# A third gate group by seven products, stick-breaking weights as products of sigmoids, and projections ahead of merges in one two-layer decoder kernel

## The chip, the cores and the metric

The kernel runs on one core of one Trainium2 chip. Such a core has a matrix engine (TensorE, PE in the profile; PEld are its weight loads), a vector engine (VectorE, DVE), a scalar engine with function tables (ScalarE, ACT), GpSimd (POOL), and SyncE (SP), which issues most DMAs. The metric is the device time of one execution in microseconds, and a lower one is better. The time before is the median of three runs.

## The reference

Two layers, each of a half-step feed-forward, a mixing of three branches, and a second half-step feed-forward, on 512 positions of width 1024. The mixing, cut to what matters here:

```python
def _stick_breaking_attention(q, k, v):            # 8 heads of 64
    z = einsum('bhqd,bhkd->bhqk', qb, k) * scale
    mask = key_pos[None, :] < q_pos[:, None]
    log_beta = log_sigmoid(z)
    log_not = where(mask, log_beta - z, 0.0)
    log_between = cumsum(log_not, axis=3, reverse=True) - log_not
    w = where(mask, exp(log_beta + log_between), 0.0)
    return w @ v

u = rmsnorm(h, mix_pre_g[l])
q_sb, k_sb, v_sb, q_fx, k_fx, v_fx, f_logit, q_mem = split(u @ w_in[l], ...)
o_sb = stick_breaking(q_sb, k_sb, v_sb)
log_f = log_sigmoid(f_logit + b_forget[l])
o_fx = forgetting(q_fx, k_fx, v_fx, log_f)         # softmax(z + c_q - c_k), c = cumsum(log_f)
o_mem = memory(q_mem, k_mem, v_mem)                # 4 heads of 128 over 256 memory rows
g_sb, g_fx, g_mem = split(sigmoid(u @ w_gate[l] + b_gate[l]), 3)
merged = g_sb * (o_sb @ w_br_sb[l]) + g_fx * (o_fx @ w_br_fox[l]) + g_mem * (o_mem @ w_br_mem[l])
h = h + rmsnorm(merged @ w_out[l], mix_post_g[l])
```

In words: the weight of a key in the stick-breaking branch is sigmoid(z) at that key times the product of 1 - sigmoid(z) = sigmoid(-z) over the keys between it and the query. `log_between` is the logarithm of that product.

## The kernel before

All large products are made from two parts: an operand is split into a high and a low part in a reduced format (`split`, and the weight units with tiles `wh_` and `wl_`), and `mm3` (L216 to L218) issues high by high, high by low and low by high. A split costs a cast on ACT (L190, or L193 with a scale) and a subtraction on DVE (L191, L194). A weight unit is 128 x 1024 elements.

Some products are made by blocks instead, with seven block products in place of eight: two rows of blocks by two columns, each a round of its own (`block_units`, `ORDER`, `FIRST`), on 256 columns at a time. The feed-forwards do so, and so do the gates of the first two branches (`SETS = (0, 1)`): `block_gates` forms the sums of the rounds, `settle` adds the bias and takes a tanh (sigmoid(x) is 0.5 + 0.5 tanh(x/2)), and the result is parked in DRAM in `gsave`. `merge` later reloads a 128 x 512 piece to a tile `ga` by a DMA of POOL (L1674), multiplies it into the branch's output projection `pb` (L1681) and adds it to `merged` (L1682). The gate of the memory branch (2) is made otherwise: `mem_gate` runs plain products of 512 columns (`pg`), then a sigmoid by Exp, a minimum, Ln, a max-add and Exp (L204 to L212), and multiplies it into `merged` (L1651), to which `mem_branch` copied the projection (L1637).

What runs when in the mixing is set by a queue of jobs `Q` in the order of `Q.add`. Heads are chains of steps woven into that queue: after each step a chain says how much PE work of the queue is to go by, `("wait", us)`, before it goes on. The order: gate rounds; four memory heads (pvm, ptm) woven with the last rounds; the projections `project` (pq, pk) and `project_v` (pv), with `mem_branch`, `mem_gate` and the merges, woven with eight stick heads and then eight forgetting heads, each started W_NEXT after the one before it; the merges of branch 1; then the output projection.

A stick head has three steps: the scores into three PSUM banks `zs` (L1305) and on them the chain of ACT and DVE passes to the weights `ts` (L1310 to L1322); after W_SB0 = 12.0 us of queue the ten transposes `pts` (L1291) into banks of the same pool ("z", four banks), split to a tile; after W_SB1 = 4.7 us eight products with v, `pvs` (L1278). A forgetting head is alike: `zf` (L1349 to L1357), row maximum, Exp with sum, reciprocal and scaling (`pf`, L1359 to L1363), `ptf`, `pvf`. It needs the cumulative sums of the forget gates, `forget_cumsum` (transposes `pfl` L1438, ACT passes, a scan, copies to `cs`), which `fox_pre` scales to `qk` (L1340). The pass tiles all come from one pool of five 128 x 512 tiles (`tmp`).

The ACT passes need function tables: Tanh stands in one, Exp and Ln in another; `tables` loads one ahead of its use.

Of the kernel before, what the change touches and what calls it, by code (L numbers as in the profile page):

```python
# [17 lines left out]
P = 128  # L18
# [4 lines left out]
def kernel(  # L23
# [73 lines left out]
    begins16 = cst.tile([P, S], BF16, name="begins16")  # L97
# [19 lines left out]
    nbgate = cst.tile([P, L, 3 * ND], F32, name="nbgate")  # L117
# [3 lines left out]
    def vectors():  # L121
# [9 lines left out]
        nc.scalar.mul(nbgate[:, :, :2 * ND], bias[:, :, :2 * ND], 0.5)  # L131
        nc.scalar.mul(nbgate[:, :, 2 * ND:], bias[:, :, 2 * ND:], -1.0)
# [8 lines left out]
    def more_constants():  # L141
# [9 lines left out]
        later(nc.vector.memset(t2[:], 1.0))  # L151
        nc.gpsimd.affine_select(out=t3[:], in_=t2[:], pattern=[[-1, S]], compare_op=ALU.not_equal,
                                fill=0.0, base=S - P - 1, channel_multiplier=1)
        later(nc.vector.tensor_copy(begins16[:], t3[:]))
# [46 lines left out]

    def log1p_exp(t, z, bias=0.0):

        nc.scalar.activation(t, z, AF.Exp, bias=bias)  # L204
        nc.vector.tensor_scalar(t, t, 2.0 ** 62, None, ALU.min)
        nc.scalar.activation(t, t, AF.Ln, bias=one_t[:t.shape[0]])

    def sigmoid_neg(t, z, bias):

        log1p_exp(t, z, bias=bias)  # L210
        nc.vector.scalar_tensor_tensor(t, z, bias, t, ALU.add, ALU.max)
        nc.scalar.activation(t, t, AF.Exp, scale=-1.0)  # L212
# [325 lines left out]
    gsave = nc.dram_tensor("gsave", (2, 2, 2, P, D), F32, kind="Internal").ap()  # L538
# [756 lines left out]
    def stick_head(q, k, value, j, ot, name, ahead):  # L1295
# [5 lines left out]
        for rows, pz in zip(banks, pzs):  # L1301
# [6 lines left out]
            zr, t = pz[:, :w], tmp(f"t{name}_{rows[0][0]}")  # L1308

            nc.scalar.activation(t[:, :w], zr, AF.Abs)  # L1310
            nc.scalar.activation(t[:, :w], t[:, :w], AF.Exp, scale=-1.0)
            nc.scalar.activation(t[:, :w], t[:, :w], AF.Ln, bias=one_t[:])
            nc.vector.scalar_tensor_tensor(t[:, :w], zr, 0.0, t[:, :w], ALU.max, ALU.add)
            for i, at in rows:
                n = (i + 1) * P
                back = t[:, at + n - 1:at - 1 if at else None:-1]

                nc.vector.tensor_tensor_scan(back, begins16[:, S - 1:S - 1 - n if n < S else None:-1], back, 1e30,
                                             ALU.mult, ALU.add)
                ptile[i] = t[:, at:at + n]  # L1320
            nc.vector.tensor_tensor(t[:, :w], zr, t[:, :w], ALU.subtract)
            nc.scalar.activation(t[:, :w], t[:, :w], AF.Exp)  # L1322
# [97 lines left out]
    W_SB0, W_SB1 = 12.0, 4.7  # L1420
# [6 lines left out]
    SETS = (0, 1)  # L1427
# [27 lines left out]
    def mixing(l, src, ks, vs, values, dst):  # L1455
# [96 lines left out]
        def project(br, p):  # L1552
            base = br * 1536
            marks["before", br, p] = len(Q.jobs)
            for x, off, scale in (("q", 0, 0.125), ("k", 512, None)):
                un1 = Unit(w_in[l], 0, ND, base + off + p * P, P, f"{x}{l}_{br}_{p}")
                marks[br, p] = Q.add([un1], lambda x=x, un1=un1, scale=scale: proj((x, br, p), un1, scale))
                if (br, p, x) == (1, FOX[0], "k"):
                    Q.add([], lambda: forget_cumsum(l, st["fl"], st))
# [13 lines left out]
        def settle(br, i, j, banks=None):  # L1573

            t = st.pop(("c", i, j))
            for m in range(4):
                c = HALVES[m % 2]
                d = br * ND + 4 * j + m
                nc.scalar.activation(t[:, m // 2, c], t[:, m // 2, c] if banks is None else banks[m // 2][:, c], AF.Tanh,
                                     bias=nbgate[:, l, d:d + 1], scale=-0.5 if j else 0.5)  # L1580
            nc.scalar.dma_start(gsave[br, i, j], t[:].rearrange("p e q -> p (e q)"))

        def block_gates(br, n, uns, top):

            nm = f"g{l}_{br}"
            if n == 2:
# [18 lines left out]
            if n == 0:  # L1605
                t = st["p0", br] = stile([P, 2, S], "rs", f"c{nm}_00", F32)
                for e in range(2):
                    nc.scalar.copy(t[:, e], pts[e][:])
                return
# [17 lines left out]
        def mem_branch(dp):  # L1627
            ub = wpair(w_br_mem[l], NP, dp * 256, f"wb{l}_2_{dp}")

            def run():  # L1630
                if dp == 0:
                    st["merged"] = [stile([P, 2, S], "f", f"mg{l}_{i}", F32) for i in range(ND // 2)]
                    st["ms"] = []
                for m in range(2):
                    pb = pbank("mm", f"pb{l}_2_{2 * dp + m}")
# [351 lines left out]
```

## Time and profile before

| | |
|---|---|
| median of 3 runs | 2362.73 us (2361.63 to 2364.0) |
| profiled execution | 2364.89 us |
| its span, first to last instruction | 2362.8 us |
| granted TensorE clock, mean | 0.998 |
| stick stage of the first layer | about 510 to 660 us of the span |
| forgetting stage of the first layer | about 660 to 790 us |
| ACT table loads in the program | 18 |

The profile gives the busy time of each engine and the share of the span, a chain of work followed back from the last instruction, and for each engine what it stood idle for. A row of the timeline is: start, duration, engine, line, operation, output from inputs, shape, and the idle time before it with what ended it. Neighbouring instructions of one kind are one row with their count. Durations of products on PE overlap, so their price is read from start to start. In a row of groups stand the total and the mean duration in nanoseconds, then the idle time before them.

### The profile page before, as it was taken

How to read it: one execution, taken by the hardware profiler on the slowest of the kernel's cores; microseconds unless marked ns; L12 is line 12 of the kernel's file. 1: busy time of each engine (PE TensorE's matmuls, PEld its weight loads, DVE VectorE, ACT ScalarE, POOL GpSimd, SP SyncE). 2: the span in 40 equal slices, each digit the busy share in tenths (PEclk: the TensorE clock that was granted, in tenths of full speed). 3: DMA queues.
4: the chain of work that ended last, by engine and by line, in shares of the span. 5: the costliest groups of instructions: out<-in, count | busy, mean ns of one | idle time of the engine just before them, and what ended most of it. 6: DMA issues, size and time to landing. Idle time of an engine off the chain costs nothing.

```text
span 2362.8 us, 32037 instructions
## 1 busy us (share of the span) xinstructions
PE 2339.0 (99%) x11944; PEld 1988.2 (84%) x11944; DVE 1827.1 (77%) x2443; ACT 1483.3 (63%) x2406; POOL 261.6 (11%) x290
## 2 busy tenths in 40 slices
PE   9999999999999999999999999999999999999998
PEld 8788889988878788888888888899888887888887
DVE  8766978767887887769787679777688887866696
ACT  6665766657765465566665566656677554656574
POOL 1101101001022111101011110010011120110110
PEclk9999999999999999999999999999999999999999
DMA  8866858632223576759586767585322236876682
GB/s 244 236 179 176 225 183 247 168 100 76 85 81 98 189 221 169 189 152 261 166 220 172 188 184 233 188 235 148 107 64 81 81 99 206 224 184 179 175 226 98
DMA packets 237407, 398.03 MB, mean 168 GB/s; under 512 B 12458, under 2 KB 86466, under 8 KB 236740
## 3 DMA queue, kind: packets, MB, share of 16 engines
q1 hardware_dynamic: 197472, 312.06, 40.5%
q0 software_dynamic: 37472, 75.54, 17.6%
q10 hardware_dynamic: 2308, 8.39, 0.9%
q8 instruction: 94, 1.54, 0.3%
q14 instruction: 61, 0.50, 0.1%
HBM read 372.87 MB, written 23.07 MB: 168 GB/s over the span
## 4 chain that ended last, share of the span: by engine, by line
PE 91%; DVE 4%; ACT 2%; DMA 1%; issue 1%; POOL 0%; DVEq 0%; SPq 0%; POOLq 0%; ACTq 0%
PE ptc L216 5%; PE ptc L218 5%; PE ptc L217 5%; PE pta L216 5%; PE pta L218 5%; PE pta L217 5%; PE pdc L218 3%; PE pdc L217 3%; PE pdc L216 3%; PE pda L218 3%; PE pda L217 3%; PE pda L216 3%; PE g L216 2%; PE g L218 2%; PE g L217 2%; PE pb L216 2%
## 5 line engine op out<-in xcount | busy, mean ns | idle before, releaser
L191 DVE TENSOR_TENSOR wl_tc<-ktc,wh_tc 128x1024 fp32r<-128x1024 f32 x80 | 97.7, 1223 | 63.3 <-ACT wh_tc L190 63.1
L191 DVE TENSOR_TENSOR wl_ta<-kta,wh_ta 128x1024 fp32r<-128x1024 f32 x80 | 97.6, 1223 | 57.6 <-ACT wh_ta L190 57.5
L190 ACT CAST wh_tc<-ktc 128x1024 fp32r<-128x1024 f32 x80 | 84.1, 1054 | 67.8 <-PE ptc L218 48.0
L218 PE MATMUL pta<-wh_ta,aga 128*128 128x512 f32 x320 | 124.7, 390 | 1.6 <-DVE aga L191 1.6
L216 PE MATMUL pta<-wh_ta,aga 128*128 128x512 f32 x320 | 125.2, 392 | 0.0
L216 PE MATMUL ptc<-wh_tc,agc 128*128 128x512 f32 x320 | 125.1, 393 | 0.0
L190 ACT CAST wh_ta<-kta 128x1024 fp32r<-128x1024 f32 x80 | 84.1, 1053 | 65.3 <-PE pta L218 41.7
L218 PE MATMUL ptc<-wh_tc,agc 128*128 128x512 f32 x320 | 124.7, 390 | 0.0
L217 PE MATMUL pta<-wl_ta,aga 128*128 128x512 f32 x320 | 124.6, 389 | 0.0
L217 PE MATMUL ptc<-wl_tc,agc 128*128 128x512 f32 x320 | 124.6, 389 | 0.0
L191 DVE TENSOR_TENSOR wl_ta<-raw_ta,wh_ta 128x1024 fp32r<-128x1024 f32 x58 | 70.9, 1224 | 43.2 <-ACT wh_ta L190 43.0
L191 DVE TENSOR_TENSOR wl_tc<-raw_tc,wh_tc 128x1024 fp32r<-128x1024 f32 x56 | 68.5, 1224 | 45.3 <-ACT wh_tc L190 45.3
L190 ACT CAST wh_ta<-raw_ta 128x1024 fp32r<-128x1024 f32 x58 | 60.9, 1052 | 46.9 <-PE pta L218 38.0
L190 ACT CAST wh_tc<-raw_tc 128x1024 fp32r<-128x1024 f32 x56 | 59.0, 1053 | 47.9 <-PE ptc L218 36.6
L216 PE MATMUL ptc<-wh_tc,us_b 128*128 128x512 f32 x224 | 87.7, 391 | 0.2
L216 PE MATMUL pda<-wh_da,aa 128*128 128x512 f32 x224 | 87.5, 391 | 0.0
L216 PE MATMUL pdc<-wh_dc,ac 128*128 128x512 f32 x224 | 87.5, 391 | 0.0
L218 PE MATMUL ptc<-wh_tc,us_b 128*128 128x512 f32 x224 | 87.2, 389 | 0.0
L217 PE MATMUL ptc<-wl_tc,us_b 128*128 128x512 f32 x224 | 87.2, 389 | 0.0
L218 PE MATMUL pda<-wh_da,aa 128*128 128x512 f32 x224 | 87.2, 389 | 0.0
L217 PE MATMUL pda<-wl_da,aa 128*128 128x512 f32 x224 | 87.2, 389 | 0.0
L217 PE MATMUL pdc<-wl_dc,ac 128*128 128x512 f32 x224 | 87.2, 389 | 0.0
(613 smaller groups left out, 7930.3 us busy)
## 6 DMA issues: line engine op xcount, KB each, us to landing
raw_ta<-in_ffn_w_gate_dram SPq DMA_DIRECT2D x44, 512.0 KB, 4.5
raw_wg<-in_w_gate_dram SPq DMA_DIRECT2D x44, 512.0 KB, 3.9
raw_tc<-in_ffn_w_gate_dram SPq DMA_DIRECT2D x44, 512.0 KB, 4.2
raw_da<-in_ffn_w_down_dram SPq DMA_DIRECT2D x42, 512.0 KB, 3.8
raw_dc<-in_ffn_w_down_dram SPq DMA_DIRECT2D x42, 512.0 KB, 3.4
kta<-in_ffn_w_up_dram SPq DMA_DIRECT2D x40, 512.0 KB, 5.9
ktc<-in_ffn_w_up_dram SPq DMA_DIRECT2D x40, 512.0 KB, 6.1
raw_wo<-in_w_out_dram SPq DMA_DIRECT2D x24, 512.0 KB, 4.1
```

The costliest lines, as they stand in the source:

```text
L190: both = [nc.scalar.copy(h_ap, src)]
L191: make = lambda: nc.vector.tensor_tensor(l_ap, src, h_ap.bitcast(F32), ALU.subtract)
L216: nc.tensor.matmul(pt, lh, rh, start=start, stop=False, skip_group_check=free)
L217: nc.tensor.matmul(pt, lh, rl, start=False, stop=False, skip_group_check=free)
L218: nc.tensor.matmul(pt, ll, rh, start=False, stop=stop, skip_group_check=free)
```

## The change

It has three parts. First, `SETS` becomes (0, 1, 2): the memory branch's gates are a third group by seven products, parked in `gsave` like the others; `mem_gate`, `mem_branch` and the two helpers of their sigmoid go, and `merge(2, ...)` starts `merged` by multiplying the reloaded gate with the bank. Second, a stick head takes two sigmoids of the scores on ACT, sigmoid(-z) to `as` and sigmoid(z) to `ts`, runs a multiplying scan backwards over `as` and multiplies `ts` with it, block by block; POOL clears one column of each block. Third, the order: W_SB0 is 7.0, `project_v` stands ahead of the merges, branch 0's merges are spread otherwise over the forgetting heads, and `forget_cumsum` is called from the last stick head's chain with a table load of its own.

```diff
@@ stick_head
+        rest = [stile([P, 2, S], "rs", f"a{name}_{x}", F32) for x in range(2)]
...
-            zr, t = pz[:, :w], tmp(f"t{name}_{rows[0][0]}")
+            zr, a, t = pz[:, :w], rest[x // 2][:, x % 2], tmp(f"t{name}_{rows[0][0]}")
-            nc.scalar.activation(t[:, :w], zr, AF.Abs)
-            nc.scalar.activation(t[:, :w], t[:, :w], AF.Exp, scale=-1.0)
-            nc.scalar.activation(t[:, :w], t[:, :w], AF.Ln, bias=one_t[:])
-            nc.vector.scalar_tensor_tensor(t[:, :w], zr, 0.0, t[:, :w], ALU.max, ALU.add)
+            nc.scalar.activation(a[:, :w], zr, AF.Sigmoid, scale=-1.0)
+            nc.scalar.activation(t[:, :w], zr, AF.Sigmoid)
             for i, at in rows:
                 n = (i + 1) * P
-                back = t[:, at + n - 1:at - 1 if at else None:-1]
-                nc.vector.tensor_tensor_scan(back, begins16[:, S - 1:S - 1 - n if n < S else None:-1], back, 1e30,
+                back = a[:, at + n - 1:at:-1]
+                nc.gpsimd.memset(t[:, at + n - 1:at + n], 0.0)
+                nc.vector.tensor_tensor_scan(back, back, ends16[:, S - 2:S - n - 1 if n < S else None:-1], 0.0,
                                              ALU.mult, ALU.add)
+                nc.vector.tensor_tensor(t[:, at:at + n - 1], t[:, at:at + n - 1], a[:, at + 1:at + n], ALU.mult)
                 ptile[i] = t[:, at:at + n]
-            nc.vector.tensor_tensor(t[:, :w], zr, t[:, :w], ALU.subtract)
-            nc.scalar.activation(t[:, :w], t[:, :w], AF.Exp)
...
-    W_SB0, W_SB1 = 12.0, 4.7
+    W_SB0, W_SB1 = 7.0, 4.7
-    SETS = (0, 1)
+    SETS = (0, 1, 2)
@@ merge
+                if br == 2 and dp == 0:
+                    st["merged"] = [stile([P, 2, S], "f", f"mg{l}_{i}", F32) for i in range(ND // 2)]
...
-                    nc.vector.scalar_tensor_tensor(a[:], a[:], 1.0, banks[m][:], ALU.add, ALU.mult)
-                    nc.vector.tensor_tensor(md, md, a[:], ALU.add)
+                    nc.vector.scalar_tensor_tensor(md if br == 2 else a[:], a[:], 1.0, banks[m][:], ALU.add, ALU.mult)
+                    if br != 2:
+                        nc.vector.tensor_tensor(md, md, a[:], ALU.add)
@@ mixing
-                if (br, p, x) == (1, FOX[0], "k"):
-                    Q.add([], lambda: forget_cumsum(l, st["fl"], st))
...
-        for one in todo[0] + todo[1][:2]:
+        for one in todo[0] + todo[1] + todo[2][:3]:
             marks["tri"] = Q.add(*one)
-        for one in todo[1][2:]:
-            marks["sets"] = Q.add(*one)
+        for one in todo[2][3:]:
+            Q.add(*one)
...
+            if i in (2, 5):
+                project_v(*heads[4 if i == 2 else 6])
+                marks.setdefault("forget", len(Q.jobs))
             if br == 0:
-                mem_branch(i)
-                for dp in ((0,), (1,), (), (2, 3))[i]:
-                    mem_gate(dp)
+                marks["mem"] = merge(2, w_br_mem, i)
             else:
-                if i == NP:
-                    marks["sb"] = len(Q.jobs)
-                merge(0, w_br_sb, i - NP)
-            if i in (2, 4):
-                project_v(*heads[i + 2])
+                for dp in ((0,), (1,), (), (2, 3))[i - NP]:
+                    marks.setdefault("sb", len(Q.jobs))
+                    merge(0, w_br_sb, dp)
...
-                            tables("natural_log_exp_and_others")
+                            tables("sigmoid_and_others")
...
+                    if kind == "pe" and n == NH - 1 and steps == 1:
+                        Q.until(marks["forget"])
+                        tables("natural_log_exp_and_others")
+                        yield from (("pe", x) for x in forget_cumsum(l, st["fl"], st))
+                    if kind == "pe" and steps == 2:
+                        pre(n + 1)
```

In the compiled program PE has 7944 products of 512 columns and 2980 of 256 afterwards, where it has 8328 and 2308 before; per layer that is 192 wide ones fewer and 336 narrow ones more. ACT has 20 table loads for 18. Outside the mixing the order of PE is the same in both.

The names in the excerpts below carry the layer, the branch's head pair, the head and the bank (`ts0_1_0_3` is layer 0, pair 1, head 0, row block 3) and at the end a running number. On DVE, between a stick head's scores and the splits of its transposes (`order` prints a scan as SCALAR_TENSOR_TENSOR with `begins16` or `ends16`), there stand before, from the second bank's subtraction on:

```order
L1321 TENSOR_TENSOR ts0_1_0_2_5165<-zs0_1_0_2_5151,ts0_1_0_2_5165 128x384
L191 TENSOR_TENSOR wl_wb0_2_1_0_5084<-raw_wb0_2_1_0_4736,wh_wb0_2_1_0_5083 128x1024
L1282 TENSOR_TENSOR ss0_0_1_5195<-pvs0_0_1_5186,ss0_0_1_5195 64x512
L1313 SCALAR_TENSOR_TENSOR ts0_1_0_1_5177<-zs0_1_0_1_5152,ts0_1_0_1_5177 128x384
L205 TENSOR_SCALAR ga0_2_0_5200<-ga0_2_0_5200 128x512
L194 SCALAR_TENSOR_TENSOR wl_wg0_2_1_0_5090<-raw_wg0_2_1_0_4742,wh_wg0_2_1_0_5089 128x1024
L1318 SCALAR_TENSOR_TENSOR ts0_1_0_1_5177<-begins16_75,ts0_1_0_1_5177 128x256
L1318 SCALAR_TENSOR_TENSOR ts0_1_0_1_5177<-begins16_75,ts0_1_0_1_5177 128x128
L191 TENSOR_TENSOR o0_0_0_4151<-ss0_0_1_5195,o0_0_0_4151 64x512
L1321 TENSOR_TENSOR ts0_1_0_1_5177<-zs0_1_0_1_5152,ts0_1_0_1_5177 128x384
```

In the changed kernel DVE has at that place, for the whole chain of the same head:

```order
L1305 SCALAR_TENSOR_TENSOR as0_1_0_0_5569<-as0_1_0_0_5569,ends16_75 128x511
L1307 TENSOR_TENSOR ts0_1_0_3_5573<-ts0_1_0_3_5573,as0_1_0_0_5569 128x511
L1305 SCALAR_TENSOR_TENSOR as0_1_0_0_5569<-as0_1_0_0_5569,ends16_75 128x383
L1305 SCALAR_TENSOR_TENSOR as0_1_0_1_5570<-as0_1_0_1_5570,ends16_75 128x255
L1307 TENSOR_TENSOR ts0_1_0_2_5581<-ts0_1_0_2_5581,as0_1_0_0_5569 128x383
L1307 TENSOR_TENSOR ts0_1_0_1_5591<-ts0_1_0_1_5591,as0_1_0_1_5570 128x255
L1305 SCALAR_TENSOR_TENSOR as0_1_0_1_5570<-as0_1_0_1_5570,ends16_75 128x127
L1269 TENSOR_TENSOR ss0_0_1_5609<-pvs0_0_1_5600,ss0_0_1_5609 64x512
L190 TENSOR_TENSOR wl_q0_0_3_5529<-raw_q0_0_3_5193,wh_q0_0_3_5528 128x1024
L1307 TENSOR_TENSOR ts0_1_0_1_5591<-ts0_1_0_1_5591,as0_1_0_1_5570 128x127
```

The gate passes `ga` and the gate's weight split `wl_wg` are gone from among the head's passes; a split of the next pair's query weights and the sum of the previous head's output stand there.

On ACT, at the forget gates, before (two of the last stick head's passes follow the chain's first three, `fa`):

```order
L190 CAST k_1_2_6051<-pk_1_2_6002 64x512
L1442 ACTIVATE fa_6063<-pfl_6058,bfor 8x512
L1443 ACTIVATE fa_6063<-fa_6063 8x512
L1444 ACTIVATE fa_6063<-fa_6063,one_t 8x512
L1637 COPY mg_3_5054<-pb_2_6_6076 128x512
L190 CAST k_1_2_6051<-pk_1_2_6002 64x512
L1310 ACTIVATE ts_3_1_3_6099<-zs_3_1_3_6094 128x512
L1310 ACTIVATE ts_3_1_2_6109<-zs_3_1_2_6095 128x384
L1449 CAST cs_6070<-fb_6064 8x512
```

And afterwards ACT has, behind the sigmoids of the last stick head:

```order
L1299 ACTIVATE as_3_1_1_6304<-zs_3_1_1_6302 128x384
L1300 ACTIVATE ts_3_1_1_6325<-zs_3_1_1_6302 128x384
L1685 ACT_TABLE_LOAD
L1428 ACTIVATE fa_6340<-pfl_6335,bfor 8x512
L1429 ACTIVATE fa_6340<-fa_6340 8x512
L1430 ACTIVATE fa_6340<-fa_6340,one_t 8x512
L189 CAST wh_k_1_3_6287<-raw_k_1_3_6024 128x1024
L1435 CAST cs_6347<-fb_6341 8x512
```

The forget gates moved from ahead of the last head's scores to behind them, with a table load in front.

On PE, at the last forgetting head (pair 1, head 1), before, from the larger banks' scores to the transposes:

```order
L1356 MATMUL zf0_1_1_3_7445<-k0_1_1_7201,q0_1_1_7114 128x512
L1357 MATMUL zf0_1_1_3_7445<-qk0_1_1_7328 128x512
L1356 MATMUL zf0_1_1_2_7444<-k0_1_1_7201,q0_1_1_7114 128x384
L1357 MATMUL zf0_1_1_2_7444<-qk0_1_1_7328 128x384
L1278 MATMUL pvf0_1_0_7478<-ptf0_1_0_7401,v0_1_0_0_6681 128x512
L1278 MATMUL pvf0_1_0_7478<-ptf0_1_0_7401,v0_1_0_0_6681 128x384 x2
L1278 MATMUL pvf0_1_0_7478<-ptf0_1_0_7401,v0_1_0_1_6757 128x256 x4
L1291 MATMUL ptf0_1_1_0_7494<-ident_65,pf0_1_1_0_7474 128x128
```

And afterwards, from the smallest bank's scores, which are now the last, to the transposes:

```order
L1342 MATMUL zf0_1_1_0_7596<-k0_1_1_7385,q0_1_1_7349 128x256
L1343 MATMUL zf0_1_1_0_7596<-qk0_1_1_7469 128x256
L1265 MATMUL pvf0_1_0_7632<-ptf0_1_0_7528,v0_1_0_0_6990 128x512 x2
L1265 MATMUL pvf0_1_0_7632<-ptf0_1_0_7528,v0_1_0_0_6990 128x384 x2
L1265 MATMUL pvf0_1_0_7632<-ptf0_1_0_7528,v0_1_0_1_7071 128x256 x4
L203 MATMUL pb0_1_1_7591<-o0_1_3_6493,wh_wb0_1_0_0_7294 128x512
L204 MATMUL pb0_1_1_7591<-o0_1_3_6493,wh_wb0_1_0_0_7294 128x512
L205 MATMUL pb0_1_1_7591<-o0_1_3_6493,wl_wb0_1_0_0_7295 128x512
L203 MATMUL pb0_1_1_7591<-o0_1_0_6490,wh_wb0_1_0_0_7294 128x512
L204 MATMUL pb0_1_1_7591<-o0_1_0_6490,wh_wb0_1_0_0_7294 128x512
L205 MATMUL pb0_1_1_7591<-o0_1_0_6490,wl_wb0_1_0_0_7295 128x512
L1278 MATMUL ptf0_1_1_0_7654<-ident_65,pf0_1_1_0_7628 128x128
```

The two smaller banks' scores stood further ahead before; now all four come together, and six products of the merge that stood ahead of them stand behind the eight pvf.

62 lines of the change are left out of this document (17 added, 45 removed).

## The prediction

> **What bounds the kernel now.** I read the shares of the engines first, then the chain that ended last, then TensorE's waits.
>
> ```profile
> span 2362.8 us, 32037 instructions
> PE 2339.0 (99%) x11944; PEld 1988.2 (84%) x11944; DVE 1827.1 (77%) x2443; ACT 1483.3 (63%) x2406; POOL 261.6 (11%) x290
> ...
> PE 91%; DVE 4%; ACT 2%; DMA 1%; issue 1%; POOL 0%; DVEq 0%; SPq 0%; POOLq 0%; ACTq 0%
> ```
>
> TensorE (PE) is busy nearly throughout and holds 91% of the chain. So two things count: how long its own instructions take, and the few microseconds in which it stands still. The waits of PE name the second part:
>
> ```profile
> PE ptf L1291 <- DVE pf L1363: 6.4, 4, 2.4
> PE zs L1305 <- DVE pts L191: 2.4, 4, 0.9
> PE pts L1291 <- ACT ts L1322: 2.1, 2, 1.0
> ...
> PE zf L1349 <- DVE ptf L191: 1.4, 2, 0.7
> ...
> PE pvs L1278 <- ACT mg L1637: 0.9, 2, 0.5
> PE zf L1349 <- DVE pts L191: 0.3, 2, 0.2
> ...
> PE pb L216 <- ACT o L190: 0.2, 1, 0.2
> ```
>
> (Totals over both layers, the number of times, the longest.) Three rows that lie outside the mixing are left out. What is shown is 13.7 us: 5.7 in the stick stage (zs 2.4, pts 2.1, pvs 0.9, and the 0.3 behind its last head), 7.8 in the forgetting stage (ptf 6.4, zf 1.4), and 0.2. No change to VectorE (DVE) or ScalarE (ACT) can bring more than this 13.7 while PE's own work stays.
>
> **The change part by part.**
>
> *The third gate group.* The compiled program has per layer 192 products of 512 columns fewer on PE, and 336 of 256 columns more (seven rounds of 48). Their prices stand in the timeline of before, from the start of the first to the start behind the last:
>
> ```profile
> 375.99 0.28 PE L216 MATMUL g<-us_a,wh_wg 128*128 128x256 f32 x1
> ...
> 393.26 0.40 PE L216 MATMUL pqm<-us_a,wh_qm 128*128 128x512 f32 x1
> ```
>
> ```profile
> 556.87 0.40 PE L216 MATMUL pg<-us_a,wh_wg 128*128 128x512 f32 x1
> ...
> 562.32 0.39 PE L216 MATMUL pq<-us_a,wh_q 128*128 128x512 f32 x1
> ```
>
> The first pair encloses 144 narrow products: 17.27 / 144 = 0.1199 us each. The second encloses 24 wide ones: 5.45 / 24 = 0.2271. The 0.28 and 0.39 in the rows are durations of overlapped instructions and no price. Over two layers: 384 x 0.2271 = 87.2 removed, 672 x 0.1199 = 80.6 added, so **-6.6 us**. An eighth of the columns goes, but half a wide product would be 0.1136 and a narrow one costs 0.1199, so only 7.6% of 87.2 is left.
>
> The Trainium skill ("TensorE: Matmul & The Clock Gate", section "Back-to-back issue gap") speaks against this part: it gives sustained spacings of some 81 ns at 128 columns and 131 ns at 512, and on a line between them 256 columns would cost 98 ns, three quarters of a wide product; by these figures (an estimate) the change would add 672 x 0.098 - 384 x 0.131 = 15.6 us. The trace has 0.1199 beside 0.2271, a ratio of 0.53, in the very loop that is to be repeated, and decides. The Trainium skill's other formula in that section, N/2.4 + 2.5 ns, gives 109 and 216 ns and with them -9.5.
>
> Three of the new rounds lengthen the straight piece ahead of the memory heads; the last four take the place among these heads that the second group's last four have now. What they need besides PE is seen where the first two groups run now:
>
> ```profile
> core 0: us, PE busy (x) PEld busy (x) DVE busy (x) ACT busy (x) POOL busy (x), PEclk, DMA share, GB/s
> 404.00:440.00 36.00, 36.00 (x256) 33.85 (x255) 25.87 (x26) 22.49 (x31) 5.68 (x6) 1.00 0.87 220
> 510.00:585.00 75.00, 73.81 (x355) 61.65 (x355) 56.27 (x85) 55.00 (x98) 3.23 (x6) 1.00 0.27 74
> 585.00:660.00 75.00, 74.53 (x414) 65.03 (x414) 60.68 (x98) 57.89 (x109) 13.69 (x17) 1.00 0.26 75
> ```
>
> In 404 to 440 PE is busy for all 36.00 us, with DVE at 0.72, ACT at 0.62 and the DMA engines at 0.87. So the group's combinations, parkings and fetches cost nothing there. If the DMA cover failed, its 0.13 of room says how thin it is; the fetches stand some 20 us ahead in the queue, so I price it at 0. Settling, reloading and the four `memset`s of a head are on engines with room (POOL 11%; its nearest row, a 128x128 memset, is not even on the chain). I take 0 for them.
>
> *The stick heads.* Next the cost of the chain between the score products (zs) and the transposes (pts), by lines and forms of DVE:
>
> ```profile
> L1681 DVE SCALAR_TENSOR_TENSOR ga<-ga,pb 128x512 f32<-128x512 f32 x32 | 21.2, 679 | 5.3 <-PE pb L218 2.9 <-DMA ga<-gsave 2.4
> L1318 DVE TENSOR_TENSOR_SCAN ts<-begins,ts 128x512 f32<-128x512 bf16 x16 | 19.5, 1217 | 0.1
> L1321 DVE TENSOR_TENSOR ts<-zs,ts 128x384 f32<-128x384 f32 x32 | 17.5, 548 | 0.3
> ...
> L1318 DVE TENSOR_TENSOR_SCAN ts<-begins,ts 128x384 f32<-128x384 bf16 x16 | 15.0, 935 | 0.0
> L211 DVE SCALAR_TENSOR_TENSOR ga<-pg,nbgate,ga 128x512 f32<-128x512 f32 x16 | 12.0, 749 | 3.7 <-ACT ga L206 3.6
> L1313 DVE SCALAR_TENSOR_TENSOR ts<-zs,ts 128x512 f32<-128x512 f32 x16 | 11.1, 692 | 28.2 <-ACT ts L1312 28.0
> ...
> L1651 DVE TENSOR_TENSOR mg<-mg,ga 128x512 f32<-128x512 f32 x16 | 11.0, 687 | 0.8 <-ACT ga L212 0.7
> L1318 DVE TENSOR_TENSOR_SCAN ts<-begins,ts 128x256 f32<-128x256 bf16 x16 | 10.9, 678 | 0.1
> L1321 DVE TENSOR_TENSOR ts<-zs,ts 128x512 f32<-128x512 f32 x16 | 10.8, 674 | 0.0
> ...
> L205 DVE TENSOR_SCALAR ga<-ga 128x512 f32<-128x512 f32 x16 | 6.7, 417 | 3.1 <-ACT ga L204 3.1
> L191 DVE TENSOR_TENSOR pts<-pts,pts 128x256 fp32r<-128x256 f32 x16 | 6.6, 415 | 0.1
> L1318 DVE TENSOR_TENSOR_SCAN ts<-begins,ts 128x128 f32<-128x128 bf16 x16 | 6.4, 400 | 0.0
> L191 DVE TENSOR_TENSOR pts<-pts,pts 128x128 fp32r<-128x128 f32 x16 | 4.5, 280 | 0.0
> ```
>
> Per head the max-add goes (0.692 + 2 x 0.546 = 1.78 us on DVE). The four scans stay (1.217 + 0.935 + 0.678 + 0.400 = 3.23; I take the multiplying scan at the price of the adding one). The three subtractions (1.77) become four multiplications by row block (0.67 + 0.55 + 0.42 + 0.28 = 1.92). On ACT four passes of each bank become two, and the one at the chain's end goes.
>
> In return PE leaves less room. Before, 14.1 us of PE work stand between zs and pts; now 8 zs, 8 pvs and 27 wide products. The first two are read from
>
> ```profile
> 535.60 1.45 PE L1305 MATMUL zs<-k,q 128*128 128x512 f32 x8
> ...
> 554.28 1.45 PE L1305 MATMUL zs<-k,q 128*128 128x512 f32 x8
> 555.57 1.46 PE L1278 MATMUL pvs<-pts,v 128*128 128x512 f32 x8
> 556.87 0.40 PE L216 MATMUL pg<-us_a,wh_wg 128*128 128x512 f32 x1
> ```
>
> as 1.29 + 1.30, so 2.59 + 27 x 0.2271 = 8.7 us. The chain needs 0.5 for the first bank, about 0.3 of latency, 0.49 for a sigmoid (I take the Abs pass's duration, its row is below), then 3.23 + 1.92 less seven overlaps of some 0.08: about 5.9 us, in all **6.0 to 6.5**. 2.2 to 2.7 us remain for what else stands in DVE's queue; the order puts two or three passes there, of which a weight split (1.22) is the largest. In most heads that just fits, in two or three of a layer's eight it does not.
>
> ```profile
> L1310 ACT ACTIVATE ts<-zs x48: 463/487/600, 511.4 to 1826.5; 128x384 f32<-128x384 f32 x32, 128x512 f32<-128x512 f32 x16
> ```
>
> So of the stick stage's 5.7: the wait for ACT's last pass (2.1) and that for the copy of the memory branch (0.9) go with their instructions. The waits for a free z bank (2.4 + 0.3) arose where the splits of pts stood behind the gates' passes on DVE, which are gone, while a reload-and-multiply and a weight split remain: I take half, 1.35. For new waits ahead of pts: nothing at the least; at the most, if every head misses by one weight split less the room, about 1.2 x 16 = 19. I take 0.3 us at three heads a layer, about 1.65 in all, since DVE's load hardly rises. Before, a head lasts 18.7 us (its zs start at 535.60 and 554.28) with DVE at 0.78, the mean of the two windows above: 14.6 us. Without the plain gates (8 a layer, so one a head, of 24 wide products) it lasts 18.7 - 5.45 = 13.2, and on DVE go 1.78 - 0.15 in the head itself, 0.42 + 0.75 + 0.69 of the gate and about 1.2 for its weight split, while 0.68 comes: 10.6, a load of 0.80. Sum 3.0, so **-2.7 us**.
>
> *The forget gates.* They run after the last stick head's sigmoids, with one table load of 1.28 us more a layer on ACT.
>
> ```profile
> 646.12 0.60 PE L1438 MATMUL pfl<-ident,fl 128*8 128x128 f32 x4
> ...
> 657.07 0.49 DVE L1340 TENSOR_SCALAR qk<-cs,sel 40x512 fp32r<-40x512 f32 x1 [1.44 <-POOL cs L1452]
> ```
>
> The chain from pfl to the scaled cumulative sums takes 11.4 us now; 12.7 with the table load, and the order leaves 17.8 us of PE work up to the first zf that needs it. Cost 0, with some 4 to 5 us of cover; without it every us counts.
>
> *The forgetting stage and its end.* Before, the last head's largest two banks are computed right ahead of only seven pvf, and then PE stands:
>
> ```profile
> 783.17 1.22 PE L1278 MATMUL pvf<-ptf,v 128*128 128x512 f32 x7
> 786.77 2.04 PE L1291 MATMUL ptf<-ident,pf 128*128 128x128 f32 x10 [2.39 <-DVE pf L1363]
> ```
>
> Now all four banks come in one piece, the largest first, and eight pvf (1.3) and six wide products (1.36) stand between the last zf and ptf, 2.66 us in place of some 1.1. So ptf's wait falls by about 1.6 to 1.7 a layer; I take 6.4 to 3.0 for both layers. The gap ahead of zf of one other head gets shorter (2.0 us for 3.4), so zf goes from 1.4 to 2.4. Together **-2.4 us**; bounds: nothing gained, and 7.8.
>
> *Sum.* -6.6 - 2.7 - 2.4 = -11.7. Against the profiled execution (2364.89, its span 2362.8) that gives 2353.2; this execution lies 2.2 above the median, so 2362.73 - 11.7 = **2351.0 us**.
>
> **The rivals.**
> R1: *the waits only move.* Denser stick heads wait as long as the old ones: 13.7 stays, only -6.6 counts: 2356.1. For it: PE's room per head falls from 14.1 to 8.7 us. Against it: two of the waits lose their cause.
> R2: *all mixing waits go*: -6.6 - 13.7 = -20.3, 2342.4. The order leaves PE too little room for that at the end of the forgetting stage.
> R3, slower: *VectorE becomes the bound of the stick heads.* Where the other passes between zs and the last multiplication exceed 2.5 us (two weight splits are 2.44), PE waits for the rest. With three splits a head needs 6.2 + 3.7 = 9.9 against 8.7, 1.2 us in each of 16 heads: +19 - 6.6 - 3.0 for the two vanished waits + the rest unchanged = +9.6, so 2372. It decides from the third split a head (the longer scan, if its product form were slower, works the same way). For it: DVE at 0.81 in 585 to 660 with PE already at 0.99. Against it: the order shows one split, rarely two.
> R4: *narrow products cost another price.* At half a wide one -10.9 in place of -6.6: 2346.7. At three quarters, if each were held up by its weight load, 672 x 0.170 - 87.2 = +27 in place of -6.6: 2385. The 144 products at 0.1199 speak against both, against the second so far that I give it nothing.
> R5: *the forget gates come late*, by 3 us a layer: 2357.
>
> That the change doesn't do what it says I leave out: the compiled order has the seven rounds and no wide gate product.
>
> **How the numbers follow.** Forecast 0.55 (2347 to 2355), R1 0.22, R2 0.06, R3 0.09, R4 0.03, R5 0.05. A measurement of this kernel can tell about 0.2% from no change, 4.7 us: faster is below 2358.0, slower above 2367.5. The forecast, R2 and R4 are faster, 0.64; of R1 and R5 (0.27) I give 0.15 to faster and 0.12 to the same; R3 is slower, 0.09. The range of 8 in 10 reaches from R2's edge, 2343, past R1 and R5 to 2361, where one half of the stick stage's bound of +19 would lead.
>
> **What would show it.** PE's count of products with the same prices per product: -6.6. In PE's waits no row of pts for ACT's last pass, none of pvs for mg; zs for pts at about 1.3; a row of pts for the DVE multiplication or the scan, near 1.7 (many times that is R3); ptf for pf near 3.0. No row of zf for qk (that is R5). The forecast is wrong if pts waits for DVE by over 5 us, if the straight gate rounds show PE idle for a DMA or a bank, or if rows of PE outside the mixing move.

## The result, and the profile after

The changed kernel takes 2344.87 us (median of four runs, 2344.13 to 2345.96), the kernel before 2363.36 us beside it (2361.63 to 2365.38): a ratio of 0.9922, 95% interval 0.9905 to 0.9939. That is 18.5 us less. Forecast were 2351.0 us, 11.7 less, in a range of 2343 to 2361. The profiled execution took 2344.36 us. So the time lies in the range, but below the 2347 to 2355 that the forecast itself had, and the gain is 1.6 times the one forecast.

The page of the changed kernel, its span, its engines and the chain that ended last:

```profile
span 2342.6 us, 32676 instructions
PE 2325.9 (99%) x12232; PEld 1994.7 (85%) x12232; DVE 1814.8 (77%) x2407; ACT 1431.0 (61%) x2307; POOL 279.5 (12%) x378
...
PE 93%; DVE 3%; DMA 2%; ACT 1%; issue 1%; SPq 0%; POOL 0%; DVEq 0%; ACTq 0%; POOLq 0%
```

PE is the bound as before, and its share of the chain has grown. Its waits in the changed kernel (total of both layers, times, longest):

```profile
PE zf L1335 <- DVE ptf L190: 3.3, 2, 2.2
PE ptf L1278 <- DVE pf L1349: 3.0, 2, 1.5
...
PE zf L1343 <- POOL qk L1324: 0.2, 1, 0.2
```

(The four rows left out lie outside the stretch that is measured below.) Of the rows of the mixing, the four of the stick stage are gone altogether; the forgetting stage keeps 6.5 us. The windows of the changed kernel over the first layer's straight gate rounds and over its stick stage (columns as in the prediction's table of windows: length, then busy us of PE, PEld, DVE, ACT and POOL, then PEclk, DMA share, GB/s):

```profile
404.00:440.00 36.00, 36.00 (x257) 33.89 (x256) 25.93 (x27) 22.86 (x32) 5.47 (x5) 1.00 0.95 232
...
550.00:662.00 112.00, 112.00 (x612) 97.58 (x611) 92.02 (x153) 68.90 (x130) 15.66 (x53) 1.00 0.31 86
```

PE stands still in neither. The DMA engines are at 0.95 in the gate rounds, where they were at 0.87, and it still costs PE nothing. DVE is at 0.82 in the stick stage, as worked out (0.80).

Where the time went is read from the first product of the memory queries (pqm) to the first of the output projection (pwo), which takes in the mixing but for its first three gate rounds; the work between is the same but for the change. The timeline of the kernel before (its pqm starts at 393.26, a row in the prediction), then that of the changed one:

```profile
808.54 0.39 PE L216 MATMUL pwo<-wh_wo,ms 128*128 128x512 f32 x1
```

```profile
392.90 0.40 PE L203 MATMUL pqm<-us_a,wh_qm 128*128 128x512 f32 x1
...
798.17 0.39 PE L203 MATMUL pwo<-wh_wo,ms 128*128 128x512 f32 x1
```

In the first layer 808.54 - 393.26 = 415.28 us become 405.27; in the second 414.83 become 403.72. Together 21.1 us are gained, and 0.9 us are lost again outside. (These are the two profiled executions, 20.2 us apart in span; the medians are 18.5 apart.) Of the 21.1 the products account for 6.6, as in the prediction (the median spacing of a product in the changed kernel is 0.227 and 0.120 us, as before). So 14.5 us came from PE's pauses and what goes with them, where 5.1 were forecast and the rows of waits show only 13.7 - 6.5 = 7.2.

### The profile page after: what moved, and what is told of

Its sections match the earlier page's. It is cut to its first block, busy times and chain, and to the rows that moved or that the text cites. A ratio compares the mean times of both kernels' runs of the same rounds, so it can differ in the third digit from the quotient of the medians.

```text
span 2342.6 us, 32676 instructions
## 1 busy us (share of the span) xinstructions
PE 2325.9 (99%) x12232; PEld 1994.7 (85%) x12232; DVE 1814.8 (77%) x2407; ACT 1431.0 (61%) x2307; POOL 279.5 (12%) x378
## 4 chain that ended last, share of the span: by engine, by line
PE 93%; DVE 3%; DMA 2%; ACT 1%; issue 1%; SPq 0%; POOL 0%; DVEq 0%; ACTq 0%; POOLq 0%
PE ptc L203 5%; PE ptc L205 5%; PE ptc L204 5%; PE pta L203 5%; PE pta L205 5%; PE pta L204 5%; PE g L203 3%; PE g L205 3%; PE g L204 3%; PE pdc L203 3%; PE pdc L205 3%; PE pdc L204 3%; PE pda L204 3%; PE pda L205 3%; PE pda L203 3%; PE pb L204 1%
```

## The experiments

Five kernels make a ladder from the one to the other; times in us, the mixing from pqm to pwo for both layers:

| kernel | median | span | mixing, layer 1 and 2 |
|---|---|---|---|
| before | 2363.36 | 2362.8 | 415.28, 414.83 |
| new stick chain alone (e12) | 2351.81 | 2349.8 | 408.94, 408.97 |
| and the third group, W_SB0 at 7, old places (e5) | 2348.59 | 2346.4 | 408.25, 406.44 |
| and the new places: the changed kernel | 2344.87 | 2342.6 | 405.27, 403.72 |
| and branch 0's merges combined later (e8) | 2341.45 | 2339.4 | 403.19, 402.71 |

The runs are from several chips; the kernel before took 2362.8 to 2363.7 us beside each of them. Spans and mixings are of one profiled execution each: a second one of the changed kernel has 406.49 and 404.17, 1.7 us more, so that steps of 1 or 2 us in this table say little.

**The new stick chain alone.** The first such run (e9) and one with one more table load a layer (e12).

```diff
 stick_head as in the changed kernel, W_SB0 = 12.0, forget_cumsum behind the last stick head
-        log1p_exp(t, z, bias=bias)
-        nc.vector.scalar_tensor_tensor(t, z, bias, t, ALU.add, ALU.max)
-        nc.scalar.activation(t, t, AF.Exp, scale=-1.0)
+        nc.scalar.activation(t, z, AF.Tanh, bias=bias, scale=0.5)      # bias and w_br scaled by 0.5
...
-                    nc.vector.tensor_tensor(md, md, a[:], ALU.mult)
+                    nc.vector.scalar_tensor_tensor(md, a[:], 1.0, md, ALU.add, ALU.mult)
...
+                        tables("exp_and_others")               # behind forget_cumsum
...
+                if n == 2 * NH - 4:                            # e12 alone
+                    tables("natural_log_exp_and_others")
```

> The kernel before with the new stick chain alone: W_SB0 at 12.0, all places and the plain products of the third gate as before. That gate's sigmoid is here one tanh on ACT and one multiplication on DVE, since the table of Exp and Ln is not loaded in the stick stage, and the forget gates run behind the last stick head as in the changed kernel. It keeps the wide gate products, so PE's work is that of before. Theory 'the chain removes the stick stage's waits and the third group is worth its products, 6.6 us, no more': the rows of zs, pts and pvs (5.7 us) go, the end of the forgetting stage stays as before (ptf 2.4 a layer, with or without the lower clock): span 2352 to 2357, and 6 to 8 us above the run with the old places (2346.4), which has the same chain and nearly the same order with the third group. Rival 'the third group also removes waits, since its gate passes no longer stand in DVE's queue': zs for pts stays at 2 us or more, span 2357 to 2362.

> The run with the new chain alone again, with one table load more a layer (Exp and Ln, ahead of the fifth forgetting head), so that the norms behind the mixing find the table that they find in the kernel before. In the first such run PE waited 10.9 us for fb and 4.5 for us_b between the mixing and the feed-forward, where the table of Exp alone was left in. Theory 'those 15 us came from table loads there': both rows go, the mixings stay at 409.0 and 407.8 us from the first pqm to the first pwo, and the span is 2349 to 2352. Rival 'they came from the mixing's end': the rows stay, span above 2365.

e9 took 2375.86 us, 12.5 more than the kernel before, and so missed every expectation of its total. Its waits of PE, and ACT's timeline between the mixing and the feed-forward:

```profile
PE utb L669 <- DVE fb L659: 10.9, 4, 3.9
PE ptf L1289 <- DVE pf L1360: 5.6, 4, 2.4
PE pgc L215 <- DVE us_b L194: 4.5, 2, 2.3
```

```profile
837.12 1.28 ACT L558 ACT_TABLE_LOAD   x1
838.42 0.29 ACT L558 ACTIVATE nhb<-nhb,eps_t 128x1 f32<-128x1 f32 x1
838.73 1.28 ACT L563 ACT_TABLE_LOAD   x1
840.02 0.20 ACT L563 ACTIVATE nhb<-nhb 128x1 f32<-128x1 f32 x1
```

The norms behind the mixing take a logarithm and an exponential in turn. With the table of Exp alone left in, each step loads its own: 50 loads in the program. With the one load of e12 it has 24, both rows go, and the time is 2351.81 us, ratio 0.9952 (0.9935 to 0.9968). So the rise came from the table that was left in, not from the mixing, and the chain without the third group brings 11.0 us in the median, 12.2 us in the two mixings. Its waits of PE in the mixing, but for 0.3 us of pb:

```profile
PE ptf L1289 <- DVE pf L1360: 5.8, 4, 2.4
```

The rows of zs, pts, pvs and both of zf are gone although the wide gates still run in the stick stage. (Their sigmoid is shorter here than in the kernel before, and the forget gates stand behind the last stick head; what part these two have in it was not tried apart.)

**The places.**

```diff
-            if i in (2, 5):
-                project_v(*heads[4 if i == 2 else 6])
-                marks.setdefault("forget", len(Q.jobs))
...
-                for dp in ((0,), (1,), (), (2, 3))[i - NP]:
-                    marks.setdefault("sb", len(Q.jobs))
-                    merge(0, w_br_sb, dp)
+                marks.setdefault("sb", len(Q.jobs))
+                merge(0, w_br_sb, i - NP)
+            if i in (2, 4):
+                project_v(*heads[i + 2])
+                marks.setdefault("forget", len(Q.jobs))
```

> The changed kernel with the projections of v behind the merges at heads 2 and 4 and one merge of branch 0 for each pair of forgetting heads, as before; gates, stick chain and W_SB0 as changed. PE then has the old end of the forgetting stage: the last head's scores in two parts, and seven pvf between the larger banks' scores and ptf. Theory 'the order at the end brings the fox stage's part': ptf waits 2.4 us again in each layer, the clock falls to 0.5 for 3.4 us behind it, and the span is 2 x (2.4 - 1.5 + 1.7), about 5 us, above that of the changed kernel, at most 8 with slow transposes. Rival 'the place of the merges is irrelevant, the gates and the chain bring all': within 2 us of the changed kernel's span of 2342.6, no clock below 1.0 in the mixing.

Measured: 2348.59 us, a span of 2346.4, 3.8 above the changed kernel. Its waits of PE in the mixing:

```profile
PE ptf L1278 <- DVE pf L1349: 5.2, 4, 2.4
PE zf L1335 <- DVE ptf L190: 2.5, 3, 1.4
```

The wait of 2.4 us at the end is back in both layers, and the span is nearer to the theory's 5 us than to the rival's 2. The mixings are 5.7 us longer than in the changed kernel. Of these, the rows give 1.4 (ptf 2.2 and pb 0.2 more, zf 1.0 less, POOL's share with it), and 3.4 are the clock, which fell to 0.5 twice in this execution and not in the changed kernel's: in the second layer at the end (1939.8 us), as expected, and in the first behind zf (700.8), not at its end. From e12 to e5 the third group brings only 3.2 us in the mixings though its products are 6.6 shorter; e5's zf waits 2.5 us, which e12's does not. That wait makes up most of what is missing, but W_SB0 differs too, so its cause is not shown.

**W_SB0 and the old chain.** The changed kernel with the old chain at 7.0 and 12.0, and with the new chain at 12.0.

```diff
-    W_SB0, W_SB1 = 7.0, 4.7
+    W_SB0, W_SB1 = 12.0, 4.7                 # e3, e4
 stick_head and its tables as before         # e2, e3
```

> The changed kernel with the old stick chain (Abs, Exp, Ln, max-add, adding scan, subtraction, Exp) and its table, all else as changed. Theory 'the shorter chain is what lets the gates go': the old chain needs some 9.2 us plus about 1.9 us of other DVE passes, PE has 8.7 us of work, so pts waits some 2 us in each of 16 heads: 20 to 40 us slower than the changed kernel, with rows of pts for ACT ts and zs for pts in PE's waits, and slower than the kernel before as well. Rival 'the third group does it alone': within 4 us of the changed kernel, 2341 to 2349.

> As the run with the old chain, but with W_SB0 at 12.0 as before. Theory: 5 us more of the queue stand between scores and transposes, so pts waits little at first, but the stick stage has only 8.7 us of such work a head on the average, so the queue runs dry up to its limit in the last heads: 10 to 30 us slower than the changed kernel, the waits all in the second half of the stick stage. Rival 'W_SB0 is free': within 4 us of the changed kernel.

> The changed kernel with W_SB0 at 12.0 as before, nothing else. Theory: as with the old chain at 12.0 the queue runs dry in the last stick heads, where the new chain of 6.2 us is then bare: 5 to 25 us slower than the changed kernel. Rival 'the lower number only follows the shorter chain and costs or brings nothing': within 4 us of it.

Measured: 2381.25 us (e2, 1.0075 of the kernel before, 1.0058 to 1.0092), 2389.1 (e3) and 2366.12 (e4, one execution each). PE's wait for the stick weights in e2, e3 and e4:

```profile
PE pts L1278 <- ACT ts L1309: 15.1, 10, 2.4
```

```profile
PE pts L1278 <- ACT ts L1309: 29.8, 4, 7.7
```

```profile
PE pts L1278 <- DVE ts L1307: 12.2, 4, 3.6
```

The third group without the shorter chain is 18 us slower than the kernel before, and 25 at 12.0: it takes wide gate products out of the place that hid the old chain. And at 12.0 the queue is spent early, so that two heads of each layer stand bare, with 7.2 to 7.7 us for the old chain and 2.5 to 3.6 for the new. In e2 (36 us above the changed kernel) and e4 (21) the theory held. In e3 its direction held, but 44 us is beyond the 10 to 30 expected. "In the last heads" was wrong for both: the bare ones are the fourth and the last of a layer's eight, each the second of a pair.

**The room of a head on DVE.** One pass more (e6) and three more (e7) in each stick head.

```diff
                 ptile[i] = t[:, at:at + n]
+            if x == 1:
+                for _ in range(1):                              # 3 in e7
+                    nc.vector.tensor_tensor(rest[0][:, :, :3 * P], rest[0][:, :, :3 * P], rest[0][:, :, :3 * P], ALU.max)
```

> The changed kernel with one pass more on DVE in each stick head (a maximum of a tile with itself, 768 columns, some 0.95 us), between the second and the third bank of the chain; the result is the same. The last multiplication ends 0.6 to 2.7 us ahead of the transposes in the trace of the changed kernel. Theory 'each head has this room of its own, and nothing is paid before it is used': only the head with 0.62 us pays, 0.3 us a layer, and the span stays within 2 us. Rival 'DVE is near its bound over the stage': the passes add up, 8 to 15 us.

> The same with three such passes in each stick head, some 2.85 us. Theory: seven of a layer's eight heads miss, by 0.1 to 2.2 us, by the room read from the trace 0.4 + 2.2 + 0.1 + 1.8 + 1.6 + 0.6 + 1.6 = 8.3 us a layer: 13 to 20 us above the changed kernel's span, in a row of pts for DVE ts. Rival 'DVE is near its bound': all 2.85 x 16 = 46 us. Rival 'heads overlap, so that lateness is taken up by the next wait': under 8 us.

One pass (0.94 us) raised the span to 2351.9, by 9.3 us: the theory missed, and the number lies in the rival's 8 to 15. Three raised it to 2371.2, by 28.6, between the theory and the rival (one execution each). Rows of e6, PE's wait, and DVE's timeline in the seventh head:

```profile
PE pts L1278 <- DVE ts L1307: 4.4, 6, 1.8
```

```profile
646.05 0.95 DVE L1311 TENSOR_TENSOR as<-as 128x768 f32<-128x768 f32 x1
...
648.09 1.23 DVE L190 TENSOR_TENSOR wl_q<-raw_q,wh_q 128x1024 fp32r<-128x1024 f32 x1
649.23 1.22 DVE L190 TENSOR_TENSOR wl_k<-raw_k,wh_k 128x1024 fp32r<-128x1024 f32 x1
650.37 1.22 DVE L193 SCALAR_TENSOR_TENSOR wl_wb<-raw_wb,wh_wb 128x1024 fp32r<-128x1024 f32 x1
651.50 0.28 DVE L1307 TENSOR_TENSOR ts<-ts,as 128x127 f32<-128x127 f32 x1
```

In the changed kernel none of the three splits stands ahead of that last multiplication, which ends 2.3 us ahead of the transposes. With 0.95 us more the order of DVE's queue, set when the program is built, is another, three splits come ahead of it, and PE waits 1.8 us. So the room of a head is no constant that one can spend: it holds for one order. These are the three splits of R3, which took 1.2 us for them; with the pass of 0.95 that would be 2.1. The seventh heads of the two layers make 3.6 of the 4.4 us in that row; four other heads wait for 0.15 to 0.24 us. The other rows of the mixings are 2.3 us longer than in the changed kernel, 1.2 of it for z banks, so that some 2 us of the 9.0 by which e6's two mixings are longer stand in no row. That DVE's load as such has a part in them (0.86 of 550 to 665 us, for 0.82) is not ruled out.

**The clock behind a long wait.** The kernel before with eight products of no use ahead of pvf in the head ahead of the last.

```diff
         r, rl, _ = HEAD_ROWS[j]
+        for _ in range(FILL if name.startswith("f") and name.endswith("_1_0") else 0):
+            nc.tensor.matmul(pv[:], value(0)[:, 2 * j:2 * j + 2, :].rearrange("p e c -> p (e c)"), tri_part(tri, 0, 0, 0),
+                             start=True, stop=True, skip_group_check=True)
...
+    FILL = 8
```

> The kernel before, with eight extra products of 512 columns in each layer's last-but-one forgetting head (pair 1, head 0), written to the bank that its own eight products then start anew, so that their result is dropped. Seven of them (1.59 us) stand where PE waits 2.39 us for pf. Theory 'clock': the long wait lowers the granted clock to 0.5 for 3.4 us behind it in each layer, 1.7 us lost each time; with a wait of 0.8 us the clock stays at 1.0 in 786 to 792 and the span falls by about 3 us (3.4 less one product that lies outside the wait, 0.23 a layer). Rival 'the slow products behind the wait come from late operands or weight loads': they stay slow, the span stays or rises by up to 4 us, as much as was put in.

The windows behind the wait in the kernel before, and in e1:

```profile
786.80:789.00 2.20, 2.20 (x11) 2.15 (x12) 1.18 (x3) 1.38 (x4) 0.84 (x2) 0.58 0.05 20
789.00:791.00 2.00, 2.00 (x7) 1.63 (x6) 1.52 (x4) 0.53 (x3) 2.00 (x3) 0.61 0.59 178
```

```profile
786.80:789.00 2.20, 2.12 (x13) 1.67 (x12) 1.69 (x4) 1.90 (x5) 1.65 (x3) 1.00 0.06 13
789.00:791.00 2.00, 2.00 (x12) 1.75 (x12) 0.82 (x3) 0.44 (x1) 1.24 (x2) 1.00 0.81 272
```

The granted clock stays at 1.00, 12 products in place of 7 run in the second window, and the kernel with sixteen products more has a span of 2359.5, 3.3 us less. In the median it is 2361.7 beside 2363.72, ratio 0.9992 (0.9982 to 1.0001), so that the times alone would not carry it; the clock does. Over the executions of that comparison, too, the mean clock is 0.999 or 1.000 in the ten of e1 and 0.997 to 0.999 in the thirteen of the kernel before.

**What is left at zf and ptf.** Branch 0's merges with both products ahead of both combinations, the last additions on POOL.

```diff
+                if br == 0:
+                    for m in range(2):
+                        yield from products(m, slice(early, NP))
                 for m in range(2):
...
-                    yield from products(m, slice(early, NP))
+                    if br != 0:
+                        yield from products(m, slice(early, NP))
...
-                        nc.vector.tensor_tensor(md, md, a[:], ALU.add)
+                        (nc.gpsimd if br == 0 and dp == 3 else nc.vector).tensor_tensor(md, md, a[:], ALU.add)
```

> The changed kernel with branch 0's merges in another order: both pieces' products first, then both reloaded gates multiplied and added, and the last merge's additions on POOL in place of DVE. Theory: zf's 3.3 us come from DVE waiting in its queue for a gate's reload ahead of the splits of ptf, and ptf's 3.0 at the end from four passes of the last merge ahead of the row maxima; zf falls to under 1, ptf to under 2, and the span by 2 to 5 us, to 2338 to 2341. Rival 'the waits belong to the tight place of the heads on PE': both rows stay, span within 1 us of 2342.6. If additions on POOL come too late for the next reader, pwo or ms waits instead and the span rises.

DVE at that place in the changed kernel, then in e8, and e8's only row of waits in the mixing:

```profile
695.66 1.16 DVE L190 TENSOR_TENSOR ptf<-ptf,ptf 128x512 fp32r<-128x512 f32 x2
698.73 0.69 DVE L1644 SCALAR_TENSOR_TENSOR ga<-ga,pb 128x512 f32<-128x512 f32 x1 [1.91 <-DMA ga<-gsave]
699.34 0.42 DVE L190 TENSOR_TENSOR ptf<-ptf,ptf 128x256 fp32r<-128x256 f32 x1
```

```profile
695.37 1.69 DVE L190 TENSOR_TENSOR ptf<-ptf,ptf 128x512 fp32r<-128x512 f32 x4
698.52 1.39 DVE L1648 SCALAR_TENSOR_TENSOR ga<-ga,pb 128x512 f32<-128x512 f32 x2 [1.46 <-DMA ga<-gsave]
```

```profile
PE ptf L1278 <- DVE pf L1349: 1.8, 4, 0.9
```

In the changed kernel DVE waits for a gate's reload with two splits of ptf behind it in its queue; in e8 all four are through by then. (PE issues the scores zf of that head in another order there, too, the largest bank first, so the run does not part the two; the reading rests on DVE's timeline.) The span falls to 2339.4, as the theory had it. What the additions on POOL bring by themselves was not tried. Run again on the same chip as the changed kernel:

> The changed kernel itself, on the same chip as the next: 2344 to 2346, span about 2342.6.

> The kernel with branch 0's merges combined later and the last additions on POOL, beside the changed kernel on the same chip. Theory: 2 to 4 us below the changed kernel in the median, since zf's row and half of ptf's are gone. Rival 'the two spans of 2342.6 and 2339.4 differed by chance': medians within 1 us.

2344.39 us (0.9919 of before, 0.9902 to 0.9935) and 2340.59 (0.9905, 0.9890 to 0.9919): 3.8 us apart, as the theory had it, and with no overlap between the single times (2343.09 to 2345.67, 2339.96 to 2341.44). So this version beats both kernels.

## Why the prediction was right, and where its sizes were off

- **What bounds it, and the products.** Right. 6.6 us of products, at the prices of before; the DMA cover of the gate rounds held, at 0.95.
- **The bound of 13.7 us for all waits.** This step failed: "No change to VectorE (DVE) or ScalarE (ACT) can bring more than this 13.7". 14.5 came in the profiled pair, with 6.5 of the rows still there. By the medians (18.5 in all) the changed kernel alone would not break the bound; e11 does, with the same products on PE: it is 22.8 us below the kernel before, 16.2 without the products, and 2.1 of its rows still stand. A row of waits counts the pause. Not in it are the products that run at the lower clock behind it, 1.7 us in each layer (3.4 us at 0.5), and the slower start behind each pause: pts waited 1.02 us at 666.08 before, but the spacing of that product was 1.42, 1.2 above the usual. Added up from start to start, the spacings at PE's pauses are 17.3 us above the usual before and 7.3 after, 10.0 less where the rows are 7.2 less. So of the 7.3 us by which the pauses gave more than the rows, 3.4 are the clock, 2.8 the spacing around the pauses, and about 1 stands elsewhere and was not traced.
- **The stick stage, -2.7.** The mis-sized term. The mechanism was right: the shorter chain and the cleared queue free the z banks and the weights. Of the 5.7 us all went, where 3.0 were to stay; the last multiplication ends 0.6 to 2.7 us ahead of the transposes in every head (8.7 in a layer's first), so that none of the misses that 1.65 us stood for occurred. With what else hung on the old chain, the new one is worth 12.2 us in the mixings without the third group (e12), more than the whole forecast.
- **The chain's price.** Right: its passes in the changed kernel (by groups) are the ones that were taken from the old. From the first score product to the last multiplication a head of the first layer (but for its first) takes 6.0 to 8.1 us with what else stands in DVE's queue, where PE has 8.7 to 9.2 of work; so the cover held, and in one head by 0.6 alone.

```profile
L1305 DVE TENSOR_TENSOR_SCAN as<-as,ends 128x511 f32<-128x511 f32 x16 | 19.5, 1219 | 13.4 <-ACT as L1299 13.3
...
L1307 DVE TENSOR_TENSOR ts<-ts,as 128x511 f32<-128x511 f32 x16 | 10.9, 682 | 1.0
```

- **The forgetting stage, -2.4.** ptf came out at 3.0, as taken. zf is at 3.3 for 2.4, and not for the reason given, a shorter gap on PE: in the trace the split of ptf that zf waits for stands behind a reload in DVE's queue, and in e8, where it does not, the row is gone. The stage keeps 6.5 us, where 5.4 were forecast.
- **The forget gates, 0.** Right in cost, but "some 4 to 5 us of cover" was too much. The changed kernel's timeline:

```profile
654.23 0.60 PE L1424 MATMUL pfl<-ident,fl 128*8 128x128 f32 x4
...
669.47 0.98 DVE L1326 TENSOR_SCALAR qk<-cs,sel 40x512 fp32r<-40x512 f32 x2
...
672.91 0.50 PE L1343 MATMUL zf<-qk 104*128 104x512 f32 x1 [0.16 <-POOL qk L1324]
```

  The chain took 16.2 us, 3.5 more than reckoned, since on DVE it queues behind the last stick head's own passes, weight splits and pts. Some 2.5 us were left, and the small wait at 672.91 is for POOL's copy of k.
- **The rivals.** R2, all waits vanish, gave 2342.4 and was taken at 0.06; the median lies between it and the forecast, nearer to R2, though 6.5 us of waits stayed: the price of a pause was too low in both. That the time still lies in the range is in part luck: its lower edge was R2's. R1 (the waits only move), R4 (another price of narrow products) and R5 (forget gates late) did not occur. R3 did not either, but in one head of eight it stands one pass away (e6). In e2 (2381 us) PE waits for the old chain's last pass on ACT, so that run does not show R3.

## What to carry to other kernels

Where an engine is busy 99% of the time, price a pause by the spacing of the products around it and by the granted clock behind it, not by its row among the waits alone. A shorter chain and a thinner cover belong together: the third group without the shorter chain was slower than the kernel before, and the wait number that fitted the old chain cost 21 us with the new (one execution). Ahead of spending an engine's apparent room, look at the order of its queue after the edit; 0.95 us more a head put three weight splits ahead of the one instruction that was waited for.

## What the runs showed of the hardware

The same kernel, run twice, has the same wait at the same place, and the clock falls behind it only once. The changed kernel, first run and second, the product behind the wait and the window that follows:

```profile
699.81 0.22 PE L1335 MATMUL zf<-causal,ident 128*128 128x128 bf16 x1 [2.23 <-DVE ptf L190]
...
699.80:703.50 3.70, 3.69 (x21) 3.19 (x21) 3.70 (x7) 0.58 (x1) 0.73 (x2) 1.00 0.17 36
```

```profile
699.32 0.23 PE L1335 MATMUL zf<-causal,ident 128*128 128x128 bf16 x1 [2.28 <-DVE ptf L190]
...
699.30:702.90 3.60, 3.58 (x12) 2.98 (x12) 3.33 (x6) 0.11 (x1) 0.52 (x1) 0.53 0.14 30
```

The second run's span is 1.3 us longer. The pause's length alone does not decide it; its place has a part. Every stretch at 0.5 inside a mixing lasted 3.41 us or a multiple of it, and within each trace the changes of the clock lie whole multiples of 3.41 us apart (in the kernel before the two stretches start at 787.13 and 1957.90, 343 times 3.413 apart). So each trace has a grid of windows. The last whole window on it ahead of the clock in question, in the changed kernel's first run, in its second, and in e5 at zf and at the end of the first layer:

```profile
695.70:699.12 3.42, 1.88 (x11) 1.34 (x10) 1.51 (x3) 1.69 (x4) 1.66 (x3) 1.00 0.63 177
```

```profile
695.98:699.39 3.41, 1.13 (x10) 0.76 (x8) 1.46 (x4) 1.05 (x1) 0.91 (x2) 1.00 0.31 93
```

```profile
697.39:700.80 3.41, 1.47 (x11) 1.14 (x10) 2.94 (x6) 0.00 (x0) 0.00 (x0) 1.00 0.02 7
775.90:779.31 3.41, 1.54 (x10) 1.28 (x8) 2.76 (x9) 2.50 (x9) 0.00 (x0) 1.00 0.98 398
```

Behind PE's 1.88 and 1.54 us of work the clock stayed at 1.00, behind 1.13 and 1.47 it fell to 0.5 for the next window. So a pause of 1.35 us (e5 at zf, with 0.6 us of shorter ones in the same window) brought the lower clock, and one of 2.37 us that the grid cuts in two did not. Over all fourteen traces, but for the first 30 and the last 20 us, each of the 25 windows at full clock in which PE worked for up to 1.50 us was followed by 0.5, and none of the 9391 with over 1.70; of the five in between, one was. (PE's busy time is modelled, so the edge is not exact.)

The Trainium skill ("TensorE: Matmul & The Clock Gate", section "Part 1: The HAM clock gate") has the clock set by the activity in a free-running window of 3413 ns; these runs agree with the window, and show that it need not be idle as a whole. For an estimate: a pause costs 1.7 us more, or nothing, by whether it leaves PE less than about 1.5 us of work in one window.
